# Gated recurrence with compact queries: the two heads of a key tile are multiplied in the two row halves of the array

## The chip, the cores and the metric

The kernel runs on one core of a Trainium2 chip. The metric is the time of one execution in microseconds (us). The kernel before takes 1286.13 us, the median of three runs between 1284.29 and 1288.33 us. The engines are called by these names: TensorE (PE, its weight loads PEld), VectorE (DVE), ScalarE (ACT), GpSimd (POOL) and SyncE (SP).

## The reference

Two layers of a streaming encoder are computed for 1024 positions of width 1024, in float32. Each layer normalises its input, projects it to 3492 columns, sends these through four parallel branches (A convolution, B gated recurrence, C state-space scan, D latent attention), multiplies each branch by a gate path, projects the four results back, normalises and adds. The change is in branch B alone:

```python
def hgrn2_branch(q, f_raw, v, gate, lb, norm_g):
    fgate = lbf + (1.0 - lbf) * jax.nn.sigmoid(zf)
    log_f = jnp.log(jnp.maximum(fgate, GATE_FLOOR))
    k = (1.0 - lbf) * jax.nn.sigmoid(-zf)
    def step(state, inp):          # per chunk, 4 heads of width 64
        b = jnp.cumsum(gt, axis=2)
        o_inter = jnp.einsum('bhtk,bhkv->bhtv', qt * jnp.exp(b), state)
        diff = b[:, :, :, None, :] - b[:, :, None, :, :]
        decay = masked_exp(causal, diff)
        scores = jnp.einsum('bhtk,bhsk,bhtsk->bhts', qt, kt, decay)
        o_intra = jnp.einsum('bhts,bhsv->bhtv', scores, vt)
        ...
    o = rms_norm(o, norm_g.reshape(B_HEADS, B_DV)).astype(q.dtype)
    return o.reshape(bsz, s, B_HEADS * B_DV) * jax.nn.silu(gate)
```

A score of query t and key s is a sum over 64 channels, each decayed by the product of that channel's gates between s and t. The decay is different in each channel, so it cannot be taken out of the sum.

## The kernel before, in words

**Layout of branch B.** Queries `qp`, keys `krb` and gates `fg` lie with features on the partitions: a tile of 128 partitions and 512 positions holds two heads of 64 channels (m = 0, 1), for each half of the sequence (g = 0, 1). The function `th_b` computes in chunks of 128 positions, four of them (t_) in a half.

**The levels.** The decays are brought into queries and keys by doubling. At level lev a block has u = 2^lev positions. The odd block of each pair of neighbours takes its queries, the even block its keys: at that time a query carries the gates from the start of its block to itself, a key those from behind itself to the end of its block, so that their product is the wanted score. L612 computes these scores for all pairs of a chunk (the moving operand is the queries of the odd blocks, 64 of the 128 positions), into the PSUM tile `plB` of two banks. Then L622 multiplies the queries of the odd blocks by the gate product of the even block, L623 the keys of the even blocks by that of the odd block, and L625 forms the products of the doubled blocks (`totB`). L629 copies the scores that belong to a pair from `plB` into the score tiles `amat`, under a byte mask, one copy for each two chunks. There are seven levels (u = 1 to 64), for two halves of the sequence and two layers: 28 levels, 56 copies. The scores of a position with itself come from L585 to L598.

**Both heads in one matmul.** The array sums over all 128 partitions, and these hold two heads. So the queries are kept block-diagonal in the tile `qz` of 128 partitions and two blocks of 512: block r has head r's queries on the 64 partitions of head r and zeros on the other 64. L593 clears the zeros on GpSimd, L594 writes query times gate, one instruction for each head. A matmul of L612 moves 128 columns, 64 for each head. There are 2 layers x 2 halves x 7 levels x 2 tiles x 4 chunks = 224 written matmuls; each float32 matmul appears in the trace as two instructions, so there are 448, in 56 groups (called bursts in the prediction) of eight. L622 works on the 64 partitions of one head at a time, since the two heads stand in different blocks. After the last level L637 adds the two blocks on GpSimd into `qp`, which L649 needs.

**After the levels.** For each chunk, L646 and L649 compute the output `poB` from the scores and from the state `stB`; L654 transposes the keys, L660 computes the update `pSB` of the state: four matmuls of 64 columns each, whose results lie in the upper or the lower half of the partitions by turns (the column halves of the array); L665 adds them to the state.

**Order of the work.** All streams of a layer (projections of A, B, C, D, gates, the convolution L468, the recurrence) are generators. A plan written as numbers, `PLAN`, gives each of them a stretch, and `weave` emits their steps by their places in it; the amounts of work that `th_b` yields are the steps' sizes. A scheduler then orders the instructions of each engine when the kernel is built: the order of emission is the priority, and a ready instruction can go ahead of one that is not (in the trace the products L585 of the second half run at 172.84 us, before a copy L629 of the first half at 176.53 us). Each engine runs its own list in order. While the recurrence waits, TensorE gets matmuls of the gates (L206 to L208, L334 to L336) or of the inputs of C (L217 to L223), VectorE steps of the convolution. Large tiles (`amat`, `totB`, `qz`, gates, loads) share a pool of seven buffers, `k4`. Weights come over SP's queue, gates and results go over GpSimd's queue.

Of the kernel before, what the change touches and what calls it, by code (L numbers as in the profile page):

```python
# [15 lines left out]
ALU = mybir.AluOpType  # L16
# [9 lines left out]
P = 128  # L26
S = 1024
D = 1024
# [12 lines left out]
# emission plan of a layer: stretch [start, end) of each stream and its amount of work  # L41
# [40 lines left out]
# columns of the packed per-feature parameters  # L82
# [6 lines left out]
# columns of the packed row parameters  # L89
# [5 lines left out]
def trunk_kernel(ctx, tc, x, pos, pre_g, post_g, wd, wv, w256, wo, cols, rows, pw, qb, kvb,  # L95
# [50 lines left out]
    # rotary tables, token-major: [tok, tile, 32] = cos|cos and -sin|sin  # L146
# [28 lines left out]
    def load_chunk(l, which, idx=0, spare=None):  # L175
        """hi / lo parts of a column chunk of w_in: returns per-k APs"""
# [23 lines left out]
    def proj_tok(hT, hs, ls, i, n, ps):  # L200
        """ps[tok of tile i, n] = h @ chunk"""
# [8 lines left out]
    def proj_feat(hT, hs, ls, m, ps):  # L210
        """ps[128 features of block m, 1024 tok]"""
# [28 lines left out]
    class Thread:  # L240
        """a stream of emission steps, spread over a stretch of the layer's plan"""
# [8 lines left out]
    def weave(threads, until):  # L250
        """emits the threads' steps in the order of their places in the plan"""
# [15 lines left out]
    for l in range(L):  # L267
        my, other = sides[l % 2], sides[1 - l % 2]
# [85 lines left out]
        # ================ tokens x features: v of B, dt of C ================  # L354
# [83 lines left out]
        # ================ A: convolution module ================  # L438
# [68 lines left out]
        # ================ rotary tables ================  # L507
# [24 lines left out]
        # ================ B: HGRN2 ================  # L532
# [38 lines left out]
        def th_b():  # L571
# [6 lines left out]
            for g in range(2):  # L578
                # scores of a position with itself
                ds = sm("dsB")  # L580
                qz = []
                for m in range(2):
# [3 lines left out]
                    for t_ in range(4):  # L586
                        T.matmul(ds[:, (t_ * 2 + m) * 2:(t_ * 2 + m) * 2 + 2], pr[:, t_ * P:(t_ + 1) * P], bon,
                                 start=True, stop=True)
                    # queries of the two heads side by side, block-diagonal over the partitions
                    z = k4("qz", (P, 2, 512))  # L590
                    for r in range(2):
                        rs = slice(r * 64, r * 64 + 64)
                        G.memset(z[rs, 1 - r, :], 0.0)  # L593
                        V.tensor_tensor(z[rs, r, :], q[rs, :], fg[m, g][rs, :], op=ALU.mult)  # L594
                    qz.append(z)
# [6 lines left out]
                for lev in range(7):  # L602
# [5 lines left out]
                    for m in range(2):  # L608
                        k_, z = kr_[m, g], qz[m]
                        for t_ in range(4):  # L610
                            o0 = (t_ * 2 + m) * P
                            T.matmul(pl[:, o0:o0 + P].rearrange("p (r b u) -> p r b u", r=2, u=u),  # L612
                                     k_[:, t_ * P:(t_ + 1) * P],
                                     z[:, :, t_ * P:(t_ + 1) * P].rearrange("p r (b o u) -> p r b o u", o=2, u=u)[:, :, :, 1, :],
                                     start=True, stop=True)
                        # double the block
                        pv = prev[m].rearrange("p (b o) -> p b o", o=2)
                        kv = k_.rearrange("p (b o u) -> p b o u", o=2, u=u)[:, :, 0, :]
                        for r in range(2):
                            rs = slice(r * 64, r * 64 + 64)  # L620
                            qv = z[rs, r, :].rearrange("p (b o u) -> p b o u", o=2, u=u)[:, :, 1, :]
                            V.tensor_tensor(qv, qv, pv[rs, :, 0].unsqueeze(2).to_broadcast([64, w // 2, u]), op=ALU.mult)  # L622
# [5 lines left out]
                    for c in range(2):  # L628
# [3 lines left out]
                            pl[:, c * 512:(c + 1) * 512].rearrange("p (a b u) -> p a b u", a=8, u=u))  # L632
# [3 lines left out]
                for m in range(2):  # L636
                    G.tensor_tensor(qp[m, g], qz[m][:, 0, :], qz[m][:, 1, :], op=ALU.add)  # L637
# [495 lines left out]
```

## Time and profile before

| | |
|---|---|
| median of 3 runs (lowest to highest) | 1286.13 us (1284.29 to 1288.33) |
| profiled execution, first to last instruction | 1287.5 us (the page gives no other time of it) |
| TensorE matmul busy | 1234.7 us, 96% |
| TensorE weight load busy | 1031.3 us, 80% |
| VectorE busy | 868.2 us, 67% |
| ScalarE busy | 458.3 us, 36% |
| GpSimd busy | 161.5 us, 13% |
| chain that ended last, by engine | PE 70%, DVE 17%, DMA 4%, issue 4% |
| mean granted TensorE clock | 0.985 |

Busy time counts an instruction from its start to its end. TensorE's matmuls overlap one another, and their ends are modelled, so its busy share is more than the share of its peak; how far apart its instructions start says more. The recurrence runs from about 117 to 300 us in layer 0 and from about 786 to 932 us in layer 1, its levels in the first part of either. A group's idle time is that of its engine right before the group's instructions, with the engine that ended it.

### The profile page before, as it was taken

The page shows a single profiled execution, that of the slowest core. Times are in us where ns is not written, and L with a number is a line of the kernel's source. Part 1 is how long each engine was busy: PE and PEld are TensorE (multiplying, and loading weights), DVE is VectorE, ACT ScalarE, POOL GpSimd, SP SyncE. Part 2 cuts the span into 40 slices and gives each one's busy share as a digit, 9 for nine tenths or more (in the row PEclk, how much of TensorE's full clock was granted, in tenths as well). Part 3 has the DMA queues.
Part 4 walks back from the last instruction along what each step waited for, and adds up shares of the span by engine and source line. Part 5 has one row for each costly group of instructions (what it writes and reads, how often), then busy time and mean ns, then how long its engine had stood idle before and what let it go on. Part 6 is the DMA issues. An engine that isn't in the chain of part 4 may idle for free.

```text
span 1287.5 us, 18437 instructions
## 1 busy us (share of the span) xinstructions
PE 1234.7 (96%) x7158; PEld 1031.3 (80%) x7158; DVE 868.2 (67%) x1767; ACT 458.3 (36%) x1064; POOL 161.5 (13%) x255
## 2 busy tenths in 40 slices
PE   6999999999989899999999999998999998999997
PEld 5888988888978567778898889897888875778786
DVE  5474799999766565536544749999996755655332
ACT  6313222122565453425432222321226645433221
POOL 2100020201122200111020000221012212001000
PEclk9999999999999989999999999999999997999999
DMA  7111122201332130144322111221124203002532
GB/s 268 34 45 53 51 82 75 74 34 48 102 101 66 57 126 10 31 158 164 101 92 66 34 66 41 74 91 42 36 71 137 90 34 109 23 18 62 168 135 78
DMA packets 33511, 101.25 MB, mean 79 GB/s; under 512 B 4512, under 2 KB 8784, under 8 KB 33424
## 3 DMA queue, kind: packets, MB, share of 16 engines
q1 hardware_dynamic: 18752, 51.42, 11.9%
q0 software_dynamic: 13808, 45.77, 11.0%
q10 hardware_dynamic: 864, 2.88, 0.6%
q8 instruction: 56, 0.92, 0.3%
q14 instruction: 31, 0.25, 0.1%
HBM read 75.11 MB, written 25.20 MB: 78 GB/s over the span
## 4 chain that ended last, share of the span: by engine, by line
PE 70%; DVE 17%; DMA 4%; issue 4%; ACT 2%; POOL 1%; DVEq 0%; SPq 0%; POOLq 0%; ACTq 0%
PE pz L959 11%; PE psc L882 6%; PE poD L898 5%; DVE ca L468 4%; PE psx L217 4%; PE psx L223 4%; PE psx L220 4%; DVE amat L629 3%; DVE qz L622 3%; PE ptp L894 3%; PE psA L217 2%; PE psA L220 2%; PE psA L223 2%; DMA lm<-acsp 2%; DVE krb L623 2%
## 5 line engine op out<-in xcount | busy, mean ns | idle before, releaser
L468 DVE SCALAR_TENSOR_TENSOR ca<-hpad,col,ca 128x512 f32<-128x512 f32 x240 | 179.8, 751 | 3.8
L173 DVE TENSOR_TENSOR wl<-raw,wh 128x1024 fp32r<-128x1024 f32 (+2 forms) x56 | 69.1, 1233 | 80.7 <-ACT wh L157 80.7
L157 ACT CAST wh<-raw 128x1024 fp32r<-128x1024 f32 (+2 forms) x56 | 57.5, 1027 | 156.3 <-PE psx L220 43.4
L206 PE MATMUL psg<-wh,hh 128*128 128x256 f32 x384 | 110.0, 287 | 0.2 <-DVE amat L598 0.2
L207 PE MATMUL psg<-wl,hh 128*128 128x256 f32 x384 | 109.2, 284 | 0.0
L208 PE MATMUL psg<-wh,hl 128*128 128x256 f32 x384 | 108.9, 284 | 0.0
L882 PE MATMUL psc<-kT,qTt 96*128 96x512 f32 (+3 forms) x192 | 82.8, 542 | 0.1
L898 PE MATMUL poD<-vD,pT 128*128 128x64 f32 x576 | 78.4, 275 | 0.9 <-ACT pT L157 0.4
L898 PEld LDWEIGHTS poD<-vD,pT 128*128 128x128 f32 x576 | 72.6, 192 | 7.4 <-DVE pT L157 0.9
L959 PE MATMUL pz<-woh,yh 128*128 128x512 f32 x240 | 76.8, 401 | 1.4 <-DVE zt L1011 1.4
L959 PE MATMUL pz<-wol,yh 128*128 128x512 f32 x240 | 76.1, 397 | 0.0
L959 PE MATMUL pz<-woh,yl 128*128 128x512 f32 x240 | 76.0, 396 | 0.0
L206 PEld LDWEIGHTS psg<-wh,hh 128*128 128x128 f32 x384 | 72.4, 188 | 0.9 <-DVE amat L598 0.4
L207 PEld LDWEIGHTS psg<-wl,hh 128*128 128x128 f32 x384 | 72.4, 189 | 0.2
L208 PEld LDWEIGHTS psg<-wh,hl 128*128 128x128 f32 x384 | 72.3, 188 | 0.1
L886 DVE TENSOR_REDUCE nm<-psc 128x1 f32<-128x1024 f32 (+7 forms) x64 | 48.5, 757 | 35.4 <-PE psc L884 34.2
L889 ACT ACTIVATE pe<-psc,nm 128x1024 f32<-128x1024 f32 (+7 forms) x64 | 47.3, 740 | 64.9 <-DVE nm L887 48.7
L612 PE MATMUL plB<-qz,krb 128*128 128x128 f32 x448 | 61.7, 281 | 7.1 <-DVE krb L623 6.6
L217 PE MATMUL psx<-hh,wh 128*128 128x512 f32 x192 | 62.6, 402 | 0.3 <-DVE amat L629 0.3
L612 PEld LDWEIGHTS plB<-qz,krb 128*128 128x128 f32 x448 | 54.5, 190 | 10.2 <-DVE krb L623 5.3
L157 ACT COPY gt<-psg 128x256 f32<-128x256 f32 x48 | 17.8, 371 | 125.2 <-PE psg L208 125.2
L223 PE MATMUL psx<-hh,wl 128*128 128x512 f32 x192 | 61.8, 400 | 0.0
(331 smaller groups left out, 2972.3 us busy)
## 6 DMA issues: line engine op xcount, KB each, us to landing
raw<-in_w_dram SPq DMA_DIRECT2D x44, 512.0 KB, 3.5
rawo<-in_wo_dram SPq DMA_DIRECT2D x16, 512.0 KB, 4.4
gsp<-gt POOLq DMA_DIRECT2D x24, 256.0 KB, 2.6
yt<-ysp SPq DMA_DIRECT2D x16, 384.0 KB, 4.1
gl<-gsp POOLq DMA_DIRECT2D x8, 512.0 KB, 5.0
ysp<-gl POOLq DMA_DIRECT2D x8, 512.0 KB, 3.4
lm<-acsp POOLq DMA_DIRECT2D x16, 256.0 KB, 3.9
xt<-in_x_dram POOLq DMA_DIRECT2D x8, 512.0 KB, 4.3
```

The source lines that it names most:

```text
L157: (V.tensor_copy if name in ONV else A.copy)(out_, in_)
L206: T.matmul(ps[:, :n], a, hs[k], start=(k == 0), stop=False)
L207: T.matmul(ps[:, :n], a, ls[k], start=False, stop=False)
L208: T.matmul(ps[:, :n], b, hs[k], start=False, stop=(k == KD - 1))
L217: T.matmul(ps[:, h * 512:(h + 1) * 512], w, hh[:, k, h * 512:(h + 1) * 512], start=(k == 0), stop=False)
L220: T.matmul(ps[:, h * 512:(h + 1) * 512], w, hl[:, k, h * 512:(h + 1) * 512], start=False, stop=False)
L223: T.matmul(ps[:, h * 512:(h + 1) * 512], wl, hh[:, k, h * 512:(h + 1) * 512], start=False, stop=(k == KD - 1))
L468: V.scalar_tensor_tensor(t, hp[:, k:k + 512], w[k], t, op0=ALU.mult, op1=ALU.add)
L612: T.matmul(pl[:, o0:o0 + P].rearrange("p (r b u) -> p r b u", r=2, u=u), k_[:, t_ * P:(t_ + 1) * P], z[:, :, t_ * P:(t_ + 1) * P].rearrang ...
L882: T.matmul(psc[:, c0:c1_], qTt[:, h, :], kT[h, c0 // 512][:, 0:c1_ - c0], start=True, stop=(c1_ < n))
L898: T.matmul(po[:, h * 64:(h + 1) * 64], pT[:, (j - j0) * P:(j - j0 + 1) * P], vD[j][:, h, :], start=(j == 0), stop=(j == i))
L959: T.matmul(pz[n], a[:, k, :], w[:, k, n * 512:(n + 1) * 512], start=(k == 0 and a is yh and w is wh), stop=(k == KD - 1 and a is yl))
```

## The change

The block-diagonal tile `qz` goes, with its clears and the final addition. The queries stay in `qp`, 64 channels of each head on that head's partitions, and are multiplied in place by gates and gate products, one instruction over 128 partitions where there were two over 64. Each written matmul of the scores becomes two, one for each head, whose stationary operand is 64 rows of keys (partitions 0 to 63 or 64 to 127) and whose moving operand is the 64 query columns of that head. The results of one head lie in the first bank of `plB`, of the other in the second. The score tiles `amat` are ordered by head first, so the copy of two chunks reads from both banks, in runs of 64 elements, and the places in `ds` and the reads in L646 follow. The comments of the file are gone too.

```diff
                 ds = sm("dsB")
-                qz = []
                 for m in range(2):
                     q, k_ = qp[m, g], kr_[m, g]
                     pr = tmp(512, "prB")
                     V.tensor_tensor(pr, q, k_, op=ALU.mult)
                     for t_ in range(4):
-                        T.matmul(ds[:, (t_ * 2 + m) * 2:(t_ * 2 + m) * 2 + 2], pr[:, t_ * P:(t_ + 1) * P], bon,
+                        d0 = (t_ // 2) * 8 + (t_ % 2) * 2 + m
+                        T.matmul(ds[:, d0:d0 + 8].rearrange("p (r x) -> p r x", r=2)[:, :, 0], pr[:, t_ * P:(t_ + 1) * P], bon,
                                  start=True, stop=True)
-                    z = k4("qz", (P, 2, 512))
-                    for r in range(2):
-                        rs = slice(r * 64, r * 64 + 64)
-                        G.memset(z[rs, 1 - r, :], 0.0)
-                        V.tensor_tensor(z[rs, r, :], q[rs, :], fg[m, g][rs, :], op=ALU.mult)
-                    qz.append(z)
+                    V.tensor_tensor(q, q, fg[m, g], op=ALU.mult)
                     yield 2
...
                     for m in range(2):
-                        k_, z = kr_[m, g], qz[m]
+                        k_, q = kr_[m, g], qp[m, g]
                         for t_ in range(4):
-                            o0 = (t_ * 2 + m) * P
-                            T.matmul(pl[:, o0:o0 + P].rearrange("p (r b u) -> p r b u", r=2, u=u),
-                                     k_[:, t_ * P:(t_ + 1) * P],
-                                     z[:, :, t_ * P:(t_ + 1) * P].rearrange("p r (b o u) -> p r b o u", o=2, u=u)[:, :, :, 1, :],
-                                     start=True, stop=True)
+                            for r in range(2):
+                                rs = slice(r * 64, r * 64 + 64)
+                                o0 = r * 512 + ((t_ % 2) * 2 + m) * P + (t_ // 2) * 64
+                                T.matmul(pl[:, o0:o0 + 64].rearrange("p (b u) -> p b u", u=u),
+                                         k_[rs, t_ * P:(t_ + 1) * P],
+                                         q[rs, t_ * P:(t_ + 1) * P].rearrange("p (b o u) -> p b o u", o=2, u=u)[:, :, 1, :],
+                                         start=True, stop=True)
                         pv = prev[m].rearrange("p (b o) -> p b o", o=2)
                         kv = k_.rearrange("p (b o u) -> p b o u", o=2, u=u)[:, :, 0, :]
-                        for r in range(2):
-                            rs = slice(r * 64, r * 64 + 64)
-                            qv = z[rs, r, :].rearrange("p (b o u) -> p b o u", o=2, u=u)[:, :, 1, :]
-                            V.tensor_tensor(qv, qv, pv[rs, :, 0].unsqueeze(2).to_broadcast([64, w // 2, u]), op=ALU.mult)
+                        qv = q.rearrange("p (b o u) -> p b o u", o=2, u=u)[:, :, 1, :]
+                        V.tensor_tensor(qv, qv, pv[:, :, 0].unsqueeze(2).to_broadcast([P, w // 2, u]), op=ALU.mult)
...
-                            pl[:, c * 512:(c + 1) * 512].rearrange("p (a b u) -> p a b u", a=8, u=u))
+                            pl.rearrange("p (a c b u) -> p a c b u", a=8, c=2, u=u)[:, :, c, :, :])
...
-                for m in range(2):
-                    G.tensor_tensor(qp[m, g], qz[m][:, 0, :], qz[m][:, 1, :], op=ALU.add)
...
-                        T.matmul(po[:, h * 64:(h + 1) * 64], amat[t_ // 2][:, (t_ % 2) * 4 + m * 2 + r, :],
+                        T.matmul(po[:, h * 64:(h + 1) * 64], amat[t_ // 2][:, r * 4 + (t_ % 2) * 2 + m, :],
```

## Rows read from the trace of the kernel before

**Rows 1.** The page's first part: busy us (share of the span) xinstructions.
```profile
span 1287.5 us, 18437 instructions
PE 1234.7 (96%) x7158; PEld 1031.3 (80%) x7158; DVE 868.2 (67%) x1767; ACT 458.3 (36%) x1064; POOL 161.5 (13%) x255
```

**Rows 2.** Busy time by stretch: length, PE, PEld, DVE, ACT, POOL, clock, DMA share, GB/s.
```profile
137.00:283.00 146.00, 142.40 (x1001) 128.68 (x1000) 142.74 (x264) 34.31 (x61) 22.07 (x27) 1.00 0.19 66
283.00:345.00 62.00, 62.00 (x367) 54.40 (x367) 57.61 (x91) 18.82 (x35) 6.92 (x10) 1.00 0.16 52
345.00:450.00 105.00, 93.17 (x535) 77.62 (x534) 63.68 (x206) 60.86 (x189) 27.43 (x42) 0.97 0.27 83
768.00:886.00 118.00, 112.27 (x836) 103.89 (x836) 115.42 (x216) 27.84 (x50) 20.17 (x24) 0.99 0.20 68
```

**Rows 3.** The chain of waits within 137 to 181 us, by line.
```profile
by line: DVE qz L622 22.0%; DVE amat L629 20.0%; DVE ca L468 17.9%; DVE krb L623 12.6%; issue 9.2%; DVE wl L173 5.1%; DVE totB L625 3.7%; DVE amat L598 3.2%; DVE prB L585 2.7%; PE plB L612 2.3%; PE dsB L587 1.8%; DVE qz L594 1.6%; PE psg L2
```

**Rows 4.** Instructions of tile plB (ns min/median/max), and idle us before them, times.
```profile
L612 PE MATMUL plB<-qz,krb x448: 270/275/383, 137.8 to 880.4; 128*128 128x128 f32 x150
L629 DVE COPY_PREDICATED amat<-msk,plB x56: 684/720/1374, 146.3 to 886.5; 128x512 f32<-128x512 uint8 x56
...
  DVE krb L623: 11.9, 13
  issue: 2.7, 5
...
  DVE amat L629: 0.8, 2
```

**Rows 5.** Instructions of tile qz, ns min/median/max.
```profile
L622 DVE TENSOR_TENSOR qz<-qz,totB x96: 400/421/1514, 148.6 to 885.1; 64x256 f32<-64x256 f32 x96
...
L594 DVE TENSOR_TENSOR qz<-qp,fg x16: 673/687/690, 117.2 to 831.3; 64x512 f32<-64x512 f32 x16
L622 DVE TENSOR_TENSOR qz<-qz,fg x16: 390/422/425, 140.9 to 843.8; 64x256 f32<-64x256 f32 x16
L637 POOL TENSOR_TENSOR qp<-qz x8: 1454/1526/1542, 180.7 to 885.6; 128x512 f32<-128x512 f32 x8
```

**Rows 6.** Groups by line and shape: busy us, mean ns | idle us before.
```profile
L173 DVE TENSOR_TENSOR wl<-raw,wh 128x1024 fp32r<-128x1024 f32 x44 | 55.9, 1271 | 59.5 <-ACT wh L157 59.5
...
L629 DVE COPY_PREDICATED amat<-msk,plB 128x512 f32<-128x512 uint8 x56 | 46.8, 888 | 0.1
...
L623 DVE TENSOR_TENSOR krb<-krb,totB 128x256 f32<-128x256 f32 x48 | 20.4, 426 | 0.9
```

**Rows 7.** Timeline of TensorE around a score burst: start us, us of the merged piece.
```profile
144.73 0.28 PE L208 MATMUL psg<-wh,hl 128*128 128x256 f32 x1
144.85 0.28 PE L206 MATMUL psg<-wh,hh 128*128 128x256 f32 x1
144.97 1.07 PE L612 MATMUL plB<-qz,krb 128*128 128x128 f32 x8
145.79 0.36 PE L207 MATMUL psg<-wl,hh 128*128 128x256 f32 x1
145.99 0.28 PE L208 MATMUL psg<-wh,hl 128*128 128x256 f32 x1
```

**Rows 8.** Timeline of TensorE around a state update on column halves.
```profile
841.08 0.28 PE L208 MATMUL psg<-wh,hl 128*128 128x256 f32 x1
841.28 0.45 PE L660 MATMUL pSB<-vB,ktB 128*64 128x64 f32 x8
...
841.88 0.29 PE L207 MATMUL psg<-wl,hh 128*128 128x256 f32 x1
```

**Rows 9.** Timeline of all engines from 180.5 us.
```profile
180.68 1.46 POOL L637 TENSOR_TENSOR qp<-qz 128x512 f32<-128x512 f32 x1 [2.02 <-DVE qz L622]
...
180.90 2.32 DVE L173 TENSOR_TENSOR wl<-raw,wh 128x1024 fp32r<-128x1024 f32 x1
```

**Rows 10.** Matmuls of line L660, ns min/median/max.
```profile
L660 PE MATMUL pSB<-vB,ktB x112: 221/222/271, 192.4 to 924.5; 128*64 128x64 f32 x112
```

## The prediction

> **What bounds the kernel now.** I read the page's first part, then the busy time by stretch, then the chain of waits inside the recurrence, then the two tiles that the change rewrites. The page says that TensorE is busy for 1234.7 of 1287.5 us [rows 1]. That share flatters TensorE, because its matmuls overlap, so I ask in which stretches it is *not* busy. The recurrence with its fillers runs at 137 to 283 us (layer 0) and 768 to 886 us (layer 1). There TensorE idles 146 − 142.40 = 3.6 us and 118 − 112.27 = 5.7 us, together 9.3 us, and VectorE idles hardly more (142.74 of 146, 115.42 of 118) [rows 2]. Both engines are full. The chain of waits in the first pass over the levels is almost wholly VectorE: the query scaling L622 has 22.0% of it, the score copies L629 20.0%, the convolution L468 17.9%, the key scaling L623 12.6% [rows 3]. This looks like a VectorE bound, but the reader should set it against the second column of rows 2: while the recurrence waits for VectorE, TensorE is given other projections, and the sum of its work is the same whatever their order. A faster VectorE can return only what TensorE waits. Those waits stand at the score matmuls: 11.9 us for the key scaling, 2.7 us of issue, 0.8 us for the score copies, 15.4 us in all [rows 4]. From 283 to 345 us TensorE has no idle time at all; from 345 to 450 us it has 11.8 us, with VectorE only 63.68 of 105 us busy [rows 2], so what is missing there is short chains and transfers more than VectorE's throughput. The granted clock is 0.99 to 1.00 in the stretches of the recurrence, the level of 2.4 GHz, so no term here comes from the clock.
>
> **VectorE's part.** The query scaling is 112 instructions on 64 partitions (96 and 16) [rows 5]; two become one on 128 partitions. The price of the wide form is in the key scaling, 128x256: 426 ns [rows 6] against 421 ns for the 64x256 query form [rows 5]. Partitions cost nothing, so 56 instructions go: 56 × 0.421 = 23.6 us. The first scaling L594 goes from 16 to 8 of 0.687 us: 5.5 us. GpSimd loses 16 clears and the 8 additions of 1.526 us that merge the halves [rows 5]. No matmul waited for these additions in rows 4, so I cost their end at nothing on the chain. But VectorE pays beside them: while one runs from 180.68 us, the subtraction L173 takes 2.32 us [rows 9] where its mean is 1.271 us [rows 6], 1.05 us more; the longest query scaling (1514 ns against a median of 421) [rows 5] is another such place. The eight come in four pairs, with one slowed VectorE instruction each: 4 × 1.05 = 4.2 us. VectorE's relief is 23.6 + 5.5 + 4.2 = 33.3 us, half in each layer. It is not yet time saved.
>
> The score copy reads its source in runs of 64 elements instead of 512. No row shows that form. Its bounds are the fastest and the slowest of the present copies, 684 and 1374 ns [rows 4], so 56 × (0.684 − 0.888) = −11 us to 56 × (1.374 − 0.888) = +27 us of VectorE time around the mean of 888 ns [rows 6]. I take no change, the nearest row being the copy itself, which has that spread already with a dense source; the range keeps both ends, of which the larger would use up VectorE's relief. The copy of either half now needs the last matmul of the burst (each reads both banks), up to half a burst, 0.45 us, later, 28 times; behind it in VectorE's order stand the next level's scalings. I cost it at nothing because convolution steps are interleaved there [rows 3]; uncovered it is 12.6 us. Four fewer large tiles per layer are wanted from a pool of seven; the gate reloads that could profit have no place among rows 4, so nothing. No DMA is issued earlier or later by the text, and on SP's queue nothing moves.
>
> **TensorE's part.** There are 448 score matmuls for 224 written ones, two instructions for each float32 product [rows 4], in 56 bursts of eight. Undisturbed filler matmuls start 0.12 us apart. From the last filler before a burst (144.85) to the second after it (145.99) are 1.14 us; two filler slots taken off, the burst costs 0.90 us [rows 7], and inside it the starts are (1.07 − 0.275)/7 = 0.114 us apart. After the change a burst has 16 instructions on 64 rows, with half the moving columns.
>
> The nearest row for a half array is the state update pSB, which uses *column* halves. Its eight instructions take 841.88 − 841.08 = 0.80, less 0.24, 0.56 us [rows 8]; inside, the starts are (0.45 − 0.222)/7 = 0.033 us apart [rows 8, 10]. Half the columns alone would explain 0.114/2 = 0.057 us. So two halves of the array do load at the same time. And 0.56 − 8 × 0.033 = 0.30 us is what entering and leaving the halved array costs. For row halves I take the pairing over: 16 matmuls of full-width loads, two at a time, 8 × 0.114 + 0.30 = 1.21 us, so +0.31 us a burst and 56 × 0.31 = **17.4 us more on TensorE**. Bounds: at 0.033 us each, 16 × 0.033 + 0.30 = 0.83, −4 us in all; one after the other, 16 × 0.114 + 0.30 = 2.12, +68 us. I take the pairing because pSB is written in the same order (both instructions of one half, then of the other).
>
> The trace has no load of a half of the rows. The Trainium skill, page "TensorE: Matmul & The Clock Gate", section "LDWEIGHTS (loading the stationary operand)", says that a load's time goes by its columns and not by its rows, which speaks against the change: the loads don't get shorter, there are only twice as many. By the page "TensorEngine Tiling (Array Packing)", section "Key Properties", different tiles may load and multiply in parallel but a change of tiling mode drains the engine; by the first rule alone the time would be that of the serial rival below, by the second that of my sum. The 0.30 us above is what this case shows of such a drain.
>
> **The sum**, against the profiled execution, whose page gives no time beyond its span of 1287.5 us (the median of the runs, 1286.13, is 1.4 lower): +17.4 for the bursts. Back come the 9.3 us of TensorE idling in the two stretches; the bounds are 0 and 15.4. After the recurrence VectorE, 57.61 of 62 us busy from 283 to 345 us, arrives up to 16.7 us earlier at the stages that follow, and of the 11.8 us of idling there I give back a quarter, 3 us in each layer, since VectorE is not full there; bounds 0 and 2 × 11.8 = 23.6. 1287.5 + 17.4 − 9.3 − 6 = 1289.6, and 1.4 less in terms of the median: **1288 us**, with its own range of 1279 to 1297. What is late next is TensorE itself, which then has hardly a pause from 137 to 345 us.
>
> **Rivals.** *The row halves load one after the other.* The place is each of the 56 bursts, the price +68 us. It decides from a burst of about 0.90 + (9.3 + 6)/56 = 1.17 us on; beyond that no idle time of TensorE is left to pay it. Against it speaks pSB [rows 8, 10]; for it, that column halves are not row halves. 1287.5 + 68 − 15.4, less 1.4, is 1339 us. The change then doesn't do what its words say.
>
> *VectorE does set the pace.* The chain [rows 3] and its 97% in both stretches speak for it, TensorE's equal fullness against. Then all waits at the score matmuls go and the later stages get their full share: 1287.5 + 17.4 − 15.4 − 23.6, less 1.4, is 1265 us.
>
> *Pairing holds, but nothing comes back.* The longer bursts delay the scalings that must wait for them to have read the queries, and the waits of rows 4 stay. The place is between burst and scaling at each level, the price the whole 17.4 us: 1304 us. It decides when TensorE's idling in the two stretches doesn't fall below 9.3 us.
>
> **How the numbers follow.** The forecast gets 0.41, VectorE's pace 0.29, serial loads 0.15, nothing back 0.15. The range of 1258 to 1310 us leaves out the serial case and the far end of VectorE's pace, some 2 in 10; its lower end lies 7 us under 1265 for a cheaper burst or copy, its upper end 6 over 1304. A difference under 0.3% (1282.3 to 1290.0 us) can't be told from none. Faster: 0.29 and 0.09 of the forecast's lower part, 0.38. Within 0.3%: 0.22 of the forecast. Slower: 0.10 of its upper part, 0.15 and 0.15, 0.40.
>
> **What would show it.** In the profile after, the burst between fillers should last 1.2 us and have its 16 starts about 0.057 us apart on average (0.11 means serial, and 2.1 us a burst). The query scaling should be 56 instructions of 0.43 us on 128 partitions, and no VectorE instruction of the recurrence should last a microsecond more than its kind. VectorE's busy time should be some 33 us less, TensorE's idling in the two stretches a few us. If VectorE falls by that and the time by over 20 us, my claim that TensorE is the bound was wrong; if the time rises by over 40 us, the pairing was.

## The result: 1352 us, 5% slower, and the profile after

The changed kernel takes 1352.03 us, the median of four runs (1350.98 to 1352.47), against 1287.23 us for the kernel before on the same chip: a ratio of 1.049 (95% interval 1.045 to 1.053). The prediction was 1288 us, with a range up to 1310. The profiled execution took 1352.23 us, its span is 1350.5 us. The medians of this document leave out an execution that lies over 1.5% above the fastest of its kernel, so VectorE's order alone has 1322.7 us below where an expectation says 1328.

The page's first part, to set beside [rows 1]: VectorE lost 31.2 us of work (33.3 were forecast), GpSimd 20.9 us, and TensorE is busy for 43 us more.

```profile
span 1350.5 us, 19259 instructions
PE 1278.0 (95%) x7606; PEld 1070.3 (79%) x7606; DVE 837.0 (62%) x1703; ACT 459.6 (34%) x1064; POOL 140.6 (10%) x231
```

Busy time by stretch of the recurrence, to set beside [rows 2] (length, PE, PEld, DVE, ACT, POOL, granted clock, DMA share, GB/s; the first two rows are layer 0, the last two layer 1). Two things are new. In the first pass over the levels (137 to 180 us, and 805 to 860 us) TensorE idles for 8.7 and 11.3 us, where it had hardly a gap. And the clock, 0.99 to 1.00 before, is 0.76, 0.60 and 0.78: large parts run at the lower level, 1.2 GHz. In the second pass (220 to 260 us) VectorE, full before, is busy for 26.79 of 40 us only.

```profile
137.00:180.00 43.00, 34.33 (x297) 32.04 (x296) 38.80 (x65) 6.22 (x10) 1.26 (x2) 0.76 0.09 30
220.00:260.00 40.00, 40.00 (x274) 35.87 (x273) 26.79 (x54) 5.51 (x10) 5.43 (x5) 0.60 0.20 67
805.00:860.00 55.00, 43.66 (x380) 40.55 (x379) 51.01 (x90) 8.93 (x15) 2.25 (x3) 0.78 0.09 32
860.00:932.00 72.00, 68.55 (x582) 60.19 (x580) 57.14 (x109) 14.00 (x25) 8.34 (x10) 0.98 0.21 70
```

The chain of waits within 137 to 181 us, by line, to set beside [rows 3]. The convolution step L468 went from 17.9% to 48.1%. It belongs to another branch and had been filler.

```profile
by line: DVE ca L468 48.1%; DVE amat L624 16.2%; issue 6.6%; DVE krb L618 6.1%; DVE qp L617 5.3%; DVE amat L592 3.1%; DVE totB L620 3.1%; PE plB L609 2.4%; PE psQ L223 2.1%; PE dsB L587 1.8%; PE psQ L220 1.6%; PE psg L206 1.5%; PE psg L207 
```

Tile plB, to set beside [rows 4]: the score matmuls now wait 37.4 us for the key scaling (11.9 before) and 11.9 us for issue (2.7). The last line is new: the query scaling, now in place, waits 16.3 us for matmuls that still read the queries. The copies L624 have not changed.

```profile
L609 PE MATMUL plB<-qp,krb x896: 267/272/473, 139.7 to 927.8; 64*128 64x64 f32 x180
L624 DVE COPY_PREDICATED amat<-msk,plB x56: 687/716/1362, 147.2 to 929.4; 128x512 f32<-128x512 uint8 x56
...
  DVE krb L618: 37.4, 20
  issue: 11.9, 17
...
  DVE qp L617: 16.3, 9
```

Tile qp answers [rows 5], the groups by line [rows 6]: 48 + 8 scalings on 128 partitions at some 420 ns, 8 first ones at 683 ns, the copy at 882 ns for 888.

```profile
L617 DVE TENSOR_TENSOR qp<-qp,totB x48: 410/420/459, 150.1 to 928.1; 128x256 f32<-128x256 f32 x48
...
L589 DVE TENSOR_TENSOR qp<-qp,fg x8: 679/683/691, 119.2 to 871.0; 128x512 f32<-128x512 f32 x8
L617 DVE TENSOR_TENSOR qp<-qp,fg x8: 397/420/429, 142.0 to 904.5; 128x256 f32<-128x256 f32 x8
```

```profile
L173 DVE TENSOR_TENSOR wl<-raw,wh 128x1024 fp32r<-128x1024 f32 x44 | 53.8, 1222 | 69.8 <-ACT wh L157 69.5
L624 DVE COPY_PREDICATED amat<-msk,plB 128x512 f32<-128x512 uint8 x56 | 46.1, 882 | 0.1
```

TensorE's timeline around the first burst, to set beside [rows 7]. It starts at 139.71 and the next matmul at 140.75: 1.04 us, and inside it the 16 starts are (1.11 − 0.272)/15 = 0.056 us apart. The row halves do load two at a time.

```profile
139.71 1.11 PE L609 MATMUL plB<-qp,krb 64*128 64x64 f32 x16
140.75 0.39 PE L206 MATMUL psg<-wh,hh 128*128 128x256 f32 x1
140.98 0.28 PE L207 MATMUL psg<-wl,hh 128*128 128x256 f32 x1
```

So each part does what it was priced at, and the kernel is 65 us slower. VectorE's timeline between two bursts shows where the time goes. Between the key scaling of m = 0 (150.40) and that of m = 1 (156.54) stand seven convolution steps of some 0.75 us; before, two stood there, and one between most other scalings.

```profile
150.07 0.41 DVE L617 TENSOR_TENSOR qp<-qp,totB 128x256 f32<-128x256 f32 x1
150.40 0.42 DVE L618 TENSOR_TENSOR krb<-krb,totB 128x256 f32<-128x256 f32 x1
150.73 0.74 DVE L468 SCALAR_TENSOR_TENSOR ca<-hpad,col,ca 128x512 f32<-128x512 f32 x1
151.40 0.42 DVE L620 TENSOR_TENSOR totB<-fg 128x256 f32<-128x256 f32 x1
151.73 3.89 DVE L468 SCALAR_TENSOR_TENSOR ca<-hpad,col,ca 128x512 f32<-128x512 f32 x5
155.54 0.42 DVE L617 TENSOR_TENSOR qp<-qp,totB 128x256 f32<-128x256 f32 x1
155.88 0.74 DVE L468 SCALAR_TENSOR_TENSOR ca<-hpad,col,ca 128x512 f32<-128x512 f32 x1
156.54 0.42 DVE L618 TENSOR_TENSOR krb<-krb,totB 128x256 f32<-128x256 f32 x1
```

TensorE at the same time: after the burst at 150.96 it has ten other matmuls, then waits 3.23 us for the key scaling. From 152.9 us on the granted clock is 0.5 for 20 us; the matmuls L206 to L208 that started 0.12 us apart now start 0.22 us apart.

```profile
150.96 1.11 PE L609 MATMUL plB<-qp,krb 64*128 64x64 f32 x16 [2.08 <-DVE krb L618]
...
153.15 0.42 PE L206 MATMUL psg<-wh,hh 128*128 128x256 f32 x1
153.37 0.41 PE L207 MATMUL psg<-wl,hh 128*128 128x256 f32 x1
157.01 1.97 PE L609 MATMUL plB<-qp,krb 64*128 64x64 f32 x16 [3.23 <-DVE krb L618]
```

The convolution steps of layer 0 before the first key scaling, after each of the 14 of the first pass and after each of the 14 of the second, counted in VectorE's lists as they were built:

```
before   30  0 0 2 1 1 1 1 1 1 1 1 2 0  19  0 2 1 5 0 1 1 1 1 1 1 1 1  43
after    30  0 1 7 2 5 4 4 8 1 7 3 4 1  13  0 0 0 0 0 0 0 0 0 0 0 0 0  30
```

Between the scalings of the first pass stand 47 steps, where there were 12, and in the second none are left, where there were 16. TensorE's list changed with it: the bursts of both m mostly stand together, in the later levels of the second pass with 7 to 24 other matmuls between one level and the next. The lists are written when the kernel is built, and the prediction had taken those of before for those of after.

### The profile page after: what moved, and what is told of

The parts are those of the page before. It is cut to its first block, busy times and chain, and to the rows that moved or that the text cites. A ratio compares the mean times of both kernels' runs of the same rounds, so it can differ in the third digit from the quotient of the medians.

```text
span 1350.5 us, 19259 instructions
## 1 busy us (share of the span) xinstructions
PE 1278.0 (95%) x7606; PEld 1070.3 (79%) x7606; DVE 837.0 (62%) x1703; ACT 459.6 (34%) x1064; POOL 140.6 (10%) x231
## 3 DMA queue, kind: packets, MB, share of 16 engines
q1 hardware_dynamic: 18752, 51.42, 11.4%
q0 software_dynamic: 13808, 45.77, 10.4%
## 4 chain that ended last, share of the span: by engine, by line
PE 74%; DVE 12%; issue 5%; DMA 5%; ACT 2%; POOL 1%; SPq 0%; DVEq 0%; POOLq 0%; ACTq 0%
PE pz L952 10%; PE poD L891 5%; DVE ca L468 5%; PE psc L875 4%; PE plB L609 3%; PE psx L220 3%; PE psx L217 3%; PE psx L223 3%; PE ptp L887 2%; PE psA L217 2%; PE psA L220 2%; PE psA L223 2%; PE psg L206 2%; PE psg L207 2%; PE psg L208 2%
## 5 line engine op out<-in xcount | busy, mean ns | idle before, releaser
L468 DVE SCALAR_TENSOR_TENSOR ca<-hpad,col,ca 128x512 f32<-128x512 f32 x240 | 179.7, 749 | 5.6 <-ACT ca L169 0.9
L206 PE MATMUL psg<-wh,hh 128*128 128x256 f32 x384 | 116.7, 304 | 0.2
L207 PE MATMUL psg<-wl,hh 128*128 128x256 f32 x384 | 114.4, 298 | 0.0
L208 PE MATMUL psg<-wh,hl 128*128 128x256 f32 x384 | 114.2, 298 | 0.0
L609 PE MATMUL plB<-qp,krb 64*128 64x64 f32 x896 | 79.5, 327 | 22.9 <-DVE krb L618 22.9
L609 PEld LDWEIGHTS plB<-qp,krb 64*128 64x128 f32 x896 | 71.7, 235 | 31.8 <-DVE krb L618 14.5
L206 PEld LDWEIGHTS psg<-wh,hh 128*128 128x128 f32 x384 | 78.0, 203 | 2.9 <-PE psg L208 0.3
L875 PE MATMUL psc<-kT,qTt 96*128 96x512 f32 (+3 forms) x192 | 79.4, 524 | 0.0
L207 PEld LDWEIGHTS psg<-wl,hh 128*128 128x128 f32 x384 | 78.0, 203 | 1.1
L208 PEld LDWEIGHTS psg<-wh,hl 128*128 128x128 f32 x384 | 77.8, 203 | 0.6
L220 PE MATMUL psx<-hl,wh 128*128 128x512 f32 x192 | 61.1, 397 | 0.0
```

Source lines behind the costliest of these rows:

```text
L206: T.matmul(ps[:, :n], a, hs[k], start=(k == 0), stop=False)
L207: T.matmul(ps[:, :n], a, ls[k], start=False, stop=False)
L208: T.matmul(ps[:, :n], b, hs[k], start=False, stop=(k == KD - 1))
L220: T.matmul(ps[:, h * 512:(h + 1) * 512], w, hl[:, k, h * 512:(h + 1) * 512], start=False, stop=False)
L468: V.scalar_tensor_tensor(t, hp[:, k:k + 512], w[k], t, op0=ALU.mult, op1=ALU.add)
L609: T.matmul(pl[:, o0:o0 + 64].rearrange("p (b u) -> p b u", u=u), k_[rs, t_ * P:(t_ + 1) * P], q[rs, t_ * P:(t_ + 1) * P].rearrange("p (b o ...
```

## The experiments

Two theories are set against each other. ORDER: the order in which the build put the instructions costs the time. BURST: matmuls on half the rows cost it, in any order. The table gives the time (median), the ratio to the kernel before on the same chip, and what the trace of each has in the recurrence: the stretch from the first score matmul to the last matmul into psx (the inputs of C), both layers added (before: 137.8 to 323.6 and 768.2 to 957.0 us). "Compact queries alone" is the change without the row halves. Of the stretch the table has the time at half clock (1.2 GHz), and TensorE's time, counted from one start to the next, in the score bursts and from the last other matmul to a burst ("entry").

| kernel | us | ratio, 95% | stretch | half clock | bursts | entry |
|---|---|---|---|---|---|---|
| before | 1287 to 1290 | | 374.7 | 3.4 | 54.3 | 11.9 |
| the change | 1352.0 | 1.045 to 1.053 | 433.7 | 88.7 | 89.5 | 21.4 |
| the change, both orders of before | 1302.7 | 1.006 to 1.013 | 380.0 | 13.7 | 59.2 | 10.9 |
| ... VectorE's order alone | 1322.7 | 1.022 to 1.032 | 405.0 | 44.4 | 76.6 | 14.4 |
| ... TensorE's order alone | 1306.8 | 1.012 to 1.020 | 392.8 | 20.5 | 64.8 | 15.3 |
| before, VectorE's order of after | 1320.0 | 1.020 to 1.027 | 405.5 | 37.5 | 73.6 | 10.3 |
| row halves alone, own order | 1374.0 | 1.062 to 1.069 | 462.8 | 139.9 | 96.8 | 32.8 |
| row halves alone, order of before | 1301.9 | 1.006 to 1.012 | 390.1 | 23.9 | 63.1 | 11.4 |
| compact queries alone, own order | 1271.7 | 0.981 to 0.989 | 357.2 | 0.0 | 46.6 | 6.3 |
| compact queries alone, order of before | 1269.1 | 0.981 to 0.987 | 358.4 | 0.0 | 48.2 | 6.3 |
| the change, order of compact queries | 1299.0 | 1.004 to 1.009 | 378.4 | 10.2 | 59.5 | 10.9 |
| the change, heads apart | 1330.4 | 1.029 to 1.037 | 411.3 | 30.7 | 84.9 | 11.3 |
| the change, full rows | 1317.1 | 1.018 to 1.030 | 406.5 | 0.0 | 96.5 | 6.2 |
| ScalarE fills the tile | 1272.3 | 0.986 to 0.990 | 359.4 | 0.0 | 47.3 | 5.8 |

**The order.** Orders are imposed by edges between instructions of one engine. They only fix places in its list: the counts of the engines' instructions are those of the change (TensorE 7606, VectorE 1703). First both lists of before, on the change:

```diff
+for c, n in zip(convs[l], PACE[l]):      # convolution step c behind key scaling n
+    if n > 0:
+        tc.add_manual_dep(c.ins, keys[l][n - 1].ins.name, ...)
+T.chain(tc)                              # PE_ORDER: bursts and other matmuls by turns
```

> The change whole, but with the order of the kernel before imposed: the convolution steps stand between the key scalings in VectorE's list where they stood before (one between most levels), and the bursts and the gate and input matmuls alternate in TensorE's list as before (a burst of one m, 11 to 24 other matmuls, the next burst). Theory ORDER (the loss comes from the list written when the kernel is built: scalings pushed behind 3 to 8 convolution steps, bursts merged, too few other matmuls between them): the 65 us go, 1270 to 1300 us, idle before plB for the key scaling back from 37 us to 12 or so, no stretch of 20 us or more at half clock. Theory BURST (matmuls on half the rows themselves hold TensorE up or bring its clock down, whatever stands around them): still 1335 us or more, with the half clock in the same stretches. Between the two, 1305 to 1330, both have a part.

1302.7 us, 3 us above the range of ORDER: 49 of the 65 us are the order. The waits at plB are gone (1.4 us in all), and the chain within 137 to 181 us is TensorE's alone:

```profile
  issue: 0.8, 3
  DVE ca L537: 0.4, 1
  DVE krb L687: 0.2, 1
...
  DVE qp L686: 20.7, 25
```

```profile
by line: PE psg L133 55.0%; PE plB L133 28.3%; PE psgA L133 6.7%; PE psQ L133 6.4%; PE dsB L133 3.6%; PE pct L501 0.2%
```

The 1335 us of BURST are excluded, but the kernel is 12 us above before, so something is left for the row halves. Does the order do it without the row halves? The other way round, the late steps in the kernel before:

```diff
+for c, n in zip(convs[l], PACE[l]):      # query scaling n behind convolution step c
+    if n < 28:
+        tc.add_manual_dep(heads[l][n].ins, c.ins.name, ...)
```

> The kernel before, every instruction of it, with the order of convolution steps of the changed kernel imposed on VectorE: the steps are pulled ahead of the scalings, 3 to 8 between two levels of the first pass and none left for the second pass. TensorE keeps its full-array bursts. Theory ORDER: the loss appears without any half-array matmul, 1320 to 1350 us, idle before plB for the key scaling above 30 us and stretches of half clock in the levels. Theory BURST: 1287 to 1300 us, clock as before.

1320 us, so yes: 30 us with not one half-array matmul in it. The stretches show where, length and engines as above. It is the second pass: no step is left to cover it, bursts and scalings wait for each other, TensorE is busy for two thirds, and the clock is 0.73 and 0.68. The wait for the key scaling (last line) is 14.8 us and not the 30 that ORDER expected. And the run doesn't change VectorE's list alone: TensorE's was built anew with it, and in the second pass has 80 (layer 0) and 88 (layer 1) score matmuls in a row without another between them, where the kernel before has at most 16.

```profile
235.00:267.00 32.00, 21.67 (x121) 19.56 (x122) 30.76 (x65) 0.66 (x2) 4.07 (x3) 0.73 0.16 53
...
880.00:912.00 32.00, 21.36 (x113) 18.99 (x114) 30.39 (x63) 1.46 (x4) 4.63 (x4) 0.68 0.16 57
...
  DVE krb L628: 14.8, 18
```

Which of the two lists is it? VectorE's list alone is brought back (the loop of the first diff), then TensorE's alone (its last line).

> The change whole, with the order of before imposed on VectorE's convolution steps alone; TensorE's list stays as the scheduler wrote it (the bursts of both m merged to sixteen written matmuls, few others between). It splits the 49 us that the order of both engines gave back. If VectorE's late scalings make the loss: 1303 to 1315 us, near the run with both orders. If the merged bursts make it: 1335 to 1352 us. The kernel before with late steps on VectorE alone lost 30 us, so half and half is 1320 to 1335.

> The change whole, with the order of before imposed on TensorE's bursts and gate or input matmuls alone; VectorE's list is the scheduler's, which now puts 2 to 4 convolution steps between the scalings of the first pass (1 to 8 in the change, one in the order of before) and none in the second half of the second pass. With VectorE's steps alone in the old order the time was 1328, with both 1303, with neither 1352. If the two parts add up: 1327 us. If a late list on VectorE is enough for the loss: 1340 us or more. If the TensorE list is what matters most: 1305 to 1315 us.

1322.7 us: VectorE's list gives 29 us back, TensorE's on top of it another 20. TensorE's alone gives 45 (1306.8 us), as was expected if it matters most. That is no clean test of the first pass, since VectorE's list, built anew, kept only 2 to 4 steps between most scalings there. In the second pass, though, VectorE has no step left from the fourth key scaling on, and with the bursts between other matmuls TensorE is full there at full clock:

```profile
225.00:270.00 45.00, 45.00 (x423) 41.28 (x423) 29.42 (x58) 8.06 (x16) 7.06 (x8) 1.00 0.17 59
```

So a second pass without convolution steps costs little as long as TensorE has other matmuls between its bursts. Both lists matter, they are not independent, and TensorE's seems to weigh more. What turns them round?

```diff
-o0 = (t_ * 2 + m) * P
-T.matmul(pl[:, o0:o0 + P]..., k_[:, t_ * P:(t_ + 1) * P], z[:, :, ...][:, :, :, 1, :], ...)
+for r in range(2):
+    rs = slice(r * 64, r * 64 + 64)
+    T.matmul(pl[:, o0:o0 + 64]..., k_[rs, t_ * P:(t_ + 1) * P], z[rs, r, ...][:, :, 1, :], ...)
```

> The row halves alone in the scheduler's own order: block-diagonal tile, clears and two query scalings kept, two matmuls in the row halves for each written one. Theory ORDER: it is the row halves that turn the order round (the list built has one to nine convolution steps between scalings), so the loss is here whole and without VectorE's relief: 1340 to 1370 us, idle before plB for the key scaling above 30 us, stretches of half clock. Rival: the in-place scaling of the compact queries turns it round; then about 1302 us, like the same instructions in the order of before.

1374 us, 4 us above the range: the row halves alone turn the order round, and without VectorE's relief it costs more. The same instructions in the order of before (next) take 1302 us. The compact queries alone keep the old kind of order and lose nothing by it. Why the build orders half-array matmuls so is on no trace, and stays open.

**The prices in one order.** The row halves in the kernel before (the diff just shown, with the order of before):

> The kernel before with one part of the change alone: the block-diagonal tile, its clears and the two query scalings on 64 partitions stay, and the scores become two matmuls in the row halves, with the copies and the places of the scores that follow from it. The order of before is imposed on VectorE and TensorE. This prices the bursts alone. Theory ORDER: a burst of 16 lasts about 1.04 us at full clock against 0.90 before, 56 x 0.14 = 8 us, so about 1295 us (1288 to 1305), no long half clock. Theory BURST: 1335 us or more and half clock in the levels.

And VectorE's and GpSimd's part without them, in its own order and in that of before:

```diff
-for r in range(2):
-    T.matmul(pl[:, o0:o0 + 64]..., k_[rs, ...], q[rs, ...][:, :, 1, :], ...)
+T.matmul(pl[:, o0:o0 + P], k_[:, t_ * P:(t_ + 1) * P], q[:, t_ * P:(t_ + 1) * P], ...)
```

> The change without the row halves: compact queries scaled on 128 partitions, copies of scores from 512 dense elements, and one full-array matmul of 128 rows and 128 columns for each chunk, so the scores of the two heads are summed and the output is not the reference's. The scheduler's own order. This prices VectorE's and GpSimd's part. Both theories: VectorE's busy time 30 us less, no long half clock. If TensorE is the bound, as the prediction had it, 1275 to 1290 us, TensorE idling less by at most 15 us; if VectorE paces the levels, 1250 to 1270 us.

> Compact queries with one full-array matmul for each chunk (scores of both heads summed, so the output is not the reference's), with the order of before imposed on both engines. Beside the whole change in that same order (1303 us) it prices the row halves, and beside its own order (1272 us) it tells what the imposed order costs a faster VectorE. If the row halves cost 12 us with their scalings in place as without: about 1290 us, and the imposed order eats the gain of 19 us. If the imposed order costs nothing: 1272 us, and the row halves cost 31 us.

1302, 1272 and 1269 us. The 1272 us lie between the two ranges of their expectation; 1269 says that the imposed order costs a faster VectorE nothing. In the order of before, the change is then −19 us for the compact queries and some +33 us for the row halves on top of them (ratios 0.984 and 1.009). The two don't simply add: taken the other way round, the row halves alone cost 12 us (1302), and the compact queries then give nothing more in the median (1303; −10.1 us in the stretch). With the compact queries first it is, in the stretch, −16.3 (374.7 to 358.4) and +21.6 us (358.4 to 380.0). The 21.6 are: bursts 59.2 − 48.2 = 11.0, entry 10.9 − 6.3 = 4.6, and 6.0 in other matmuls (309.9 − 303.9), where 13.7 us at half clock cost up to 6.8. That half clock stands from 211 to 224 us in the change and in the row halves alone, both in the order of before, from 214 us in the order of the compact queries, from 215 us with TensorE's order alone, from 220 us with the heads apart (below). In layer 1 the change in the order of before keeps full clock over the whole recurrence (776 to 968 us below), so half rows don't always bring it down. TensorE is not idle in layer 0 either; it had outputs and state updates, and 0.7 us before the clock fell a half-row burst began. The compact kernel, with outputs, state updates and bursts there too, keeps 1.00. The two stretches of the change in the order of before, and then the first for the compact queries in the same order:

```profile
205.00:230.00 25.00, 25.00 (x185) 22.63 (x185) 17.75 (x36) 4.46 (x9) 4.10 (x4) 0.73 0.19 64
...
776.00:968.00 192.00, 191.35 (x1434) 166.79 (x1432) 166.05 (x289) 45.20 (x77) 17.13 (x24) 1.00 0.19 63
```

```profile
205.00:230.00 25.00, 24.53 (x220) 23.89 (x217) 24.47 (x50) 4.22 (x11) 6.66 (x7) 1.00 0.18 63
```

Is that the half rows, or twice as many small matmuls? In the change with the order of before, both operands take all rows:

```diff
-k_[rs, t_ * P:(t_ + 1) * P], q[rs, t_ * P:(t_ + 1) * P]...
+k_[:, t_ * P:(t_ + 1) * P], q[:, t_ * P:(t_ + 1) * P]...
```

> The change whole in the order of before (1303 us), every instruction in number, columns and place as there, but each score matmul takes all 128 rows and not the 64 of its head (so the scores of both heads are summed in either place, and the output is not the reference's). It asks whether the half clock that the row halves brought from 211 to 224 us in three different orders, and that the full-array kernels don't have there, belongs to the half rows or to twice as many matmuls of 64 columns. Full loads don't pair, so a burst takes some 1.7 us, 56 x 0.7 = 39 us more. If the half rows bring the clock down: no half clock from 205 to 235 us, and 1303 + 39 - 7 = 1335 us. If it is the number of small matmuls: the half clock is there, for longer, and the time is 1345 us or more.

The half clock is gone (205 to 235 us below), though there are as many small matmuls and their bursts take longer. In the order of before it goes with the half rows, and not with the number of matmuls, by one trace of each. The bursts cost 37 us more (59.2 to 96.5; 39 were expected), entry and other matmuls give back 11: +26.5 us in the stretch. The median, 1317 us, is under both values of the expectation, and 12 us under the profiled execution (1329.54). The granted clock tells most of that: it is 0.983 in the profiled execution, of which 45.6 us are at half clock, all outside the stretch, and 0.991 to 0.994 in the other three, which is 16 to 24 us at half clock and so up to 11 to 15 us less time.

```profile
205.00:235.00 30.00, 30.00 (x244) 27.97 (x243) 25.13 (x46) 8.01 (x15) 4.26 (x5) 1.00 0.25 88
```

The same two kernels show the price of entering the halved array. With half rows a burst starts 154.80 − 154.59 = 0.21 us after the matmul before it, with full rows 156.69 − 156.58 = 0.11 us; some 50 such places make the 4.6 us of entry, by estimate. The Trainium skill, page "TensorEngine Tiling (Array Packing)", section "Key Properties", says that a change of tiling mode drains the engine; the 0.1 us agrees with it.

```profile
154.59 0.28 PE L133 MATMUL psg<-wl,hh 128*128 128x256 f32 x1
154.80 1.11 PE L133 MATMUL plB<-qp,krb 64*128 64x64 f32 x16
155.83 0.39 PE L133 MATMUL psg<-wh,hl 128*128 128x256 f32 x1
156.06 0.28 PE L133 MATMUL psg<-wh,hh 128*128 128x256 f32 x1
```

```profile
156.58 0.28 PE L133 MATMUL psg<-wl,hh 128*128 128x256 f32 x1
156.69 1.89 PE L133 MATMUL plB<-qp,krb 128*128 128x64 f32 x16
158.40 0.36 PE L133 MATMUL psg<-wh,hl 128*128 128x256 f32 x1
```

What is the pairing of loads worth? The loop over heads is put outside the one over chunks.

```diff
-for t_ in range(4):
-    for r in range(2):
+for r in range(2):
+    for t_ in range(4):
```

> The change whole in the order of before (1303 us), with the loop over the two heads outside the loop over the chunks: four matmuls in one row half, then four in the other, so that neighbours mostly share a half. Theory PAIRS (two loads in different halves start together, 6 to 7 ns apart, and this alone keeps a burst at 1.04 us): loads of one half come one after the other at the 0.11 us of a pair, the burst takes 1.6 to 1.9 us, and 56 of them add 30 to 45 us: 1333 to 1350 us. Rival: a load on 64 rows is short by itself; then the burst stays near 1.04 us and the time near 1303 us.

1330 us, 3 under the range of PAIRS and 27 above the rival. A burst takes 157.48 − 155.94 = 1.54 us against 1.03 in the same order and 1.71 on full rows, all at full clock: loads of one half follow each other, except where the half changes.

```profile
155.94 1.61 PE L133 MATMUL plB<-qp,krb 64*128 64x64 f32 x16
157.48 0.39 PE L133 MATMUL psg<-wh,hl 128*128 128x256 f32 x1
```

**A better version.** With the order that the build writes for compact queries, imposed on the change (the first diff, with other numbers):

> The change whole, with the order that the scheduler itself writes for compact queries and full-array matmuls imposed on VectorE's convolution steps and TensorE's bursts and gate or input matmuls. With the order of before the scalings in place waited 20.7 us for bursts that stood late in TensorE's list; this order was written for the faster VectorE. Theory ORDER: 1272 us plus 56 bursts of 16 against 8, 56 x 0.18 = 10 us: 1280 to 1290 us, which would beat both kernels by a little. If the row halves cost the clock or hold up VectorE in any order: about 1303 us, as with the order of before.

1299.0 us, a miss by 9 us: the scalings wait less (10.4 us for 20.7), but that was no part of the loss, since TensorE hardly waited in either (1.6 and 1.4 us before plB). So the row halves themselves had to go, and the compact queries to stay:

```diff
+V.tensor_tensor(q, q, fg[m, g], op=ALU.mult)        # 128 partitions, in place
+for r in range(2):
+    A.copy(z[rs, r, :], q[rs, :])
...
+V.tensor_tensor(qv, qv, pv[:, :, 0]..., op=ALU.mult)  # qv: odd blocks of q
+for r in range(2 if lev < 6 else 0):
+    A.copy(zv, qv[rs])                               # zv: odd blocks of z[rs, r]
```

> A version of its own: the compact queries of the change, scaled in place on 128 partitions, beside the full-array matmuls of before. ScalarE copies the scaled queries of each level into the two blocks of the block-diagonal tile (16 + 96 copies), whose zeros are cleared once; the last addition on GpSimd goes, since the compact queries are there. By the findings so far the row halves cost 34 us and the compact queries gain 19: this should have the gain without the cost, if ScalarE's copies (some 0.35 us each, in a stretch where it is busy for 34 of 146 us) come in time: 1265 to 1278 us. If the copies end the levels' chain (scaling, copy, next burst), the time is 1285 to 1300 us and TensorE waits for ScalarE before plB.

1272.3 us, ratio 0.988 (0.986 to 0.990): it beats the kernel before by 1.2% and the change by 80 us. ScalarE's 96 copies take 0.41 us each; they wait 28.2 us for the matmuls that read the tile, and no score matmul waits for anything.

```profile
L627 ACT COPY qz<-qp x96: 390/407/442, 141.4 to 864.1; 64x256 f32<-64x256 f32 x96
...
  PE plB L615: 28.2, 26
```

## Why the prediction was wrong

**The step that failed** is the cover of the waits. The prediction read it from the lists of before and took it over. On VectorE it cost the later copies "at nothing because convolution steps are interleaved there", at worst 12.6 us. On TensorE it held that "while the recurrence waits for VectorE, TensorE is given other projections, and the sum of its work is the same whatever their order". The change turned both lists round: the steps became what the scalings wait for, and the bursts stood together with few other matmuls between them. TensorE's idle time before the bursts, all rows of plB added, went from 16.4 us to 52.3, and is 1.4 in the order of before. In the stretch the order costs 433.7 − 380.0 = 53.7 us. 75 of its 89 us at half clock come with it, which explains at most half of 75, 37 us; the rest is waiting at the bursts. TensorE's list seems to have the larger part: alone in its old order it gives 45 us back, though VectorE's list was milder in that build too. No rival had this case, and the range ended 42 us short of it.

**"No term here comes from the clock"** failed with it: true of the trace of before, not of a kernel in which TensorE waits, nor, by the comparison of half and full rows, of this order with half-row bursts.

**VectorE's relief** was right: 31.2 us for 33.3, and both the copies and the scalings cost what was said. What it gives back was sized well too: 15.3 us (9.3 in the recurrence, 6 behind it), against 16.3 in the stretch and 19 in the median. It comes back in the recurrence more than behind it: bursts 54.3 to 48.2 and entry 11.9 to 6.3 are 11.7 us of it; outside the stretch the trace is 5.9 us shorter, with 11.8 us less at half clock. So [rows 2] understated TensorE's waiting; the waits of [rows 4], 15.4 us, were the better measure.

**The bursts** cost 11.0 + 4.6 = 15.6 us for 17.4, in a like order on compact queries. The pairing held. By the prediction's own measure, from the last filler before a burst (154.59) to the second after it (156.06) less two slots of 0.12 us, a lone burst costs 1.23 us for the 1.21 forecast; its 16 instructions alone take 1.04.

**TensorE is the bound**: right in a like order, where the chain is TensorE's alone. In the built order it fell: there TensorE waits at the bursts for what VectorE's list has put off.

**The sum** of the terms as measured in a like order is −16.3 + 15.6 + 6.0 = +5.3 us in the stretch, against +8.1 and −6 later. The medians differ by 12 us. The rest lies outside the stretch, where the time at half clock differs from trace to trace: 907 us with 23 us at half clock (compact queries, order of before), 913 with 34 (before), 917 to 926 with 43 to 46 (the change, the change in both other orders, full rows), but 906 with 23 in the change with TensorE's order alone. So the change does not always bring it on. Executions of one kernel differ in it too: the change in the order of compact queries took 1285.5 us at a granted clock of 0.992 and 1304.4 us at 0.975. At 0.988 it took 1291.7 us, the kernel before on the same chip 1284.7 to 1288.3, 3 to 7 us less, which is near the +5.3. What sets the clock of an execution stays open.

**The markers**: a rise of over 40 us was to mean that the pairing failed. It didn't; that marker had no room for an order.

## What to carry to other kernels

Where instructions are put in order when the kernel is built, a change of an instruction's shape can rewrite the lists of several engines: compare the two lists first, and price the edit in one fixed order, or a gain of 16 us and a cost of 54 can't be told apart. Where a stage has a dependent chain, filler work belongs between its steps, to the last of them, on the engine that bounds the kernel above all: drawn ahead, it delays the first half and leaves the second without cover. And when an operand's layout costs the busy engine, let an idle one make the layout before the matmuls are changed.

## What the runs showed of the chip

- Row halves of the array load in pairs where neighbours are in different halves: 16 instructions take 1.04 us in turns, 1.54 us half by half, 1.71 us on full rows. A single load of 64 rows is hardly shorter (median 0.188 us, on 128 rows 0.192).
- TensorE's clock fell to 1.2 GHz though TensorE had not been idle, from 211 to 224 us, in kernels with half-row bursts (granted clock 0.73 for 205 to 230 us); with the same matmuls on full rows it kept 1.00. That is one trace of each; in layer 1 the half-row kernel in the order of before kept 1.00 too.
- Executions of one kernel differ in the granted clock, and the time goes with it: 1285.5 us at 0.992, 1304.4 us at 0.975.
- Going from full rows to row halves costs 0.1 us before the first of them (0.21 for 0.11 us).
